# A decoder trunk on one core: an opening in a given order, and a last block that accumulates onto the turned residual stream

## The chip, the cores and the metric

The kernel runs on one core of one Trainium2 chip. The metric is device time in microseconds (us); lower is better. The core has a matrix engine (TensorE, PE in the profile, with its weight loads as PEld), a vector engine (VectorE, DVE), a scalar engine (ScalarE, ACT), GpSimd (POOL), and SyncE (SP), which here only issues transfers. Each engine executes its own list of instructions in order and waits on semaphores for the others; transfers are issued by SP, ACT or POOL and executed by 16 DMA engines. A name such as L1604 is a line of the kernel before. Line numbers in the trace of the changed kernel are its own.

## What is computed

Two layers on one sequence of 512 tokens with 1024 features. Each layer is a gated feed-forward at half weight, a mixer with three kinds of heads, and a second gated feed-forward.

```python
def rms_norm(x, gain):
    xf = x.astype(jnp.float32)
    inv = lax.rsqrt(jnp.mean(xf * xf, axis=-1, keepdims=True) + EPS)
    return (xf * inv).astype(x.dtype) * gain

def swiglu(h, w_in, w_out):
    gate, up = jnp.split(h @ w_in, 2, axis=-1)
    return (jax.nn.silu(gate) * up) @ w_out

for l in range(DEPTH):                                   # 2
    x = x + 0.5 * swiglu(rms_norm(x, ffn1_norm[l]), ffn1_w_in[l], ffn1_w_out[l])
    h = rms_norm(x, mix_norm[l]) @ w_mix_in[l]
    y = ...                                              # short convolution, HGRN2 and FoX heads
    x = x + y @ w_mix_out[l]
    x = x + 0.5 * swiglu(rms_norm(x, ffn2_norm[l]), ffn2_w_in[l], ffn2_w_out[l])
```

The feed-forward is 2816 wide (22 blocks of 128). `hgrn_lb_logits` gives each layer its lower bounds, a small softmax and cumulative sum.

## The kernel before

**Layout and precision.** The residual stream stays on the chip as `xT`, with features on the partitions: 8 slices of 128 features by 512 tokens. Every fp32 matrix product is made of three products of a faster type: an operand is split into a high part (`hi`, a cast on ACT) and a low part (`lo`, a subtraction on DVE), and `mm3` (L308 to L321) issues high by high (L312), high by low (L318) and low by high (L319) into one PSUM bank. So each block of weights passes ACT and DVE before PE can use it. `granule` (L278) loads a pair of weight blocks into `st` (two buffers) and splits them into `hl` (three buffers).

**PSUM.** There are eight banks of 128 by 512 fp32 under four tags: "mm" (3), "sc" (2), "pt" (2), "po" (1). `next4` (L254) gives a group of four in turn: mm, mm, mm, po and sc, sc, pt, pt.

**Order.** A scheduler places the instructions; where `follow` (L272) ties an instruction to the one before it on its engine, the order is as written.

**A feed-forward** (`ffn`, L416) has three parts. First, `covered` of the 22 columns are computed by full products over the 8 slices of x, in groups of two columns, gate and up. Then `halved` runs the remaining columns and two thirds of the output product with seven half-size products in place of eight, on sums of quarters of the weights (`add` and `total` make these, the former by an accumulating transfer from POOL). Last come the six remaining hidden blocks by full products, 72 products for each half of the features.

**The opening.** The first feed-forward of layer 0 covers six columns in three groups (`cover`, L478). In its first group x has to be brought in as well: `open_x` and `load_x` (L1579, L1597) load a slice of x as tokens by features, turn it by four PE transposes into PSUM (L1604), make its high and low parts times the norm's gain (L378, L379), copy it to `xT` (L1594) and add its square to `sqacc` (L389 to L393). The products of the first group do not need the norm's factor `inv`: this is multiplied in after the sum. Behind the first group `build_consts` makes masks on DVE, `lower_bounds` (L923) the lower bounds, and `norm` calls `end_norm` (L403): a product of `sqacc` with a constant matrix on PE (L405) into a bank with the tag "po", a logarithm, an exponential and a square on ACT, and three steps on DVE (L399 to L401). The second group (banks mm, mm, mm, po) needs none of it; the third uses the banks of the first, which `clear` (L529) empties with `inv`. The gain is loaded by SP as 1024 single numbers into 128 partitions (L368). The four loads of weights for the first half-size columns (L823) are issued by SP without regard to the loads of the opening.

**The end.** The last feed-forward writes the output with tokens on the partitions. `turn_x` (L1562) turns `xT` back by 32 PE transposes (L1569) into the "sc" banks, and ACT copies them to SBUF (L1574). The last 144 products go into mm, mm, mm, po and then sc, sc, pt, pt, and for each bank DVE computes 0.5 times the bank plus the turned x (L462), and SP writes 256 KB of the output (L466).

**Tables of ACT.** `table` (L258) loads a table of functions each time that it is called, 15 times in the program.

Of the kernel before, what the change touches and what calls it, by code (L numbers as in the profile page):

```python
# [23 lines left out]
P = 128  # L24
# [132 lines left out]
class Trunk:  # L157
# [8 lines left out]
    def __init__(self, ctx, tc):  # L166
# [20 lines left out]
        self.tab, self.tab_users = None, []  # L187
# [70 lines left out]
    def table(self, name):  # L258
        p = self.nc.scalar.preload_act_table_set(name)
# [18 lines left out]
    def granule(self, parts, kk, ahead=True, skew=0, keep=False):  # L278
# [48 lines left out]
    def stream_steps(self, jobs, parts_of, act, nk, mid=None, pre=None, given=None):  # L327
        k = 0
        while k < nk:
# [7 lines left out]
            rows = self.granule(parts_of(k, kk), kk, pre is None, skew, keep)  # L337
# [78 lines left out]
    def ffn(self, w_in, w_out, next_gain, covered, begin=None, out=None):  # L416
        nc = self.nc
        tc = self.tc
        with tc.tile_pool(name=self.n("ffn"), bufs=1) as fp:
# [4 lines left out]
            self.entry = {}  # L424
            halved = self.halved(fp, w_in, w_out, covered)
# [14 lines left out]
            last = out is not None  # L440
            self.ntog += 1
            if last:
                xs = self.turn_x()
            for dg in range(2):
                banks = self.next4()

                def parts(k, kk, dg=dg):
# [3 lines left out]
                spans = [slice(c, c + P) for c in (0, 128, 256, 384)]  # L451
                self.stream(
                    [
                        (bk, slice(0, T), c) if last else (bk, c, None)
                        for bk, c in zip(banks, spans)
                    ],
                    parts, lambda k: (self.hh[k // 2][:, k % 2, :], self.hl[k // 2][:, k % 2, :]), nf,
                )
                if last:
                    for i in range(4):  # L460
                        o = self.xo[dg * 4 + i]
                        nc.vector.scalar_tensor_tensor(  # L462
                            out=o, in0=banks[i], scalar=0.5, in1=xs[dg * 4 + i],
                            op0=ALU.mult, op1=ALU.add,
                        )
                        nc.sync.dma_start(out[0, spans[i], dg * T : (dg + 1) * T], o)  # L466
                    continue
# [10 lines left out]
    def cover(self, fp, w_in, covered, begin, then):  # L478
        nc = self.nc
        if begin is not None:  # L480
            x, gain, logits = begin
        for f in range(0, covered, 2):
# [8 lines left out]
            def norm():  # L491
                self.end_norm(self.bank("pt" if self.ntog % 2 == 0 else "po"), fp)
                self.xparts = self.halves_of_x(fp)

                for _ in range(2 if begin is not None else 7):
                    next(self.xparts)


            self.stream(
                [(bk, slice(c, c + P), None) for bk, c in zip(banks, (0, 256, 128, 384))],  # L500
                parts, self.xact, KD,
                (2, norm) if opening and begin is None else None,
                (lambda *a: self.open_x(x, gain, fp, *a)) if opening and begin else None,
            )
            if opening and begin is not None:
# [221 lines left out]
    def halved(self, fp, w_in, w_out, covered):  # L727
# [116 lines left out]
        for n, (kind, w, p) in enumerate(seq):  # L844
# [48 lines left out]
            else:  # L893
# [29 lines left out]
    def lower_bounds(self, logits, scratch):  # L923
# [11 lines left out]
        nc.sync.dma_start(lg, logits.rearrange("l (r p) -> p l r", p=P))  # L935
        m = take(2)
        nc.vector.tensor_copy(m, lg[:, 0, :])
# [624 lines left out]
    def turn_x(self):  # L1562
        nc = self.nc
        res, self.xo = [], []
        for h in range(2):
            for i in range(4):
                b = self.bank(("mm", "sc")[self.ntog % 2])
                for q in range(4):
                    nc.tensor.transpose(  # L1569
                        b[:, q * P : (q + 1) * P],  # L1570
                        self.xT[:, h * 4 + q, i * P : (i + 1) * P], self.ident,
                    )
                o = self.res.tile([P, 2, T], F32, tag=f"x{4 * h + i}", name=self.n("xt"))
                nc.scalar.copy(o[:, 0, :], b)  # L1574
                res.append(o[:, 0, :])
                self.xo.append(o[:, 1, :])
        return res

    def open_x(self, x, gain, fp, k, loaded=False):  # L1579
        if not loaded:  # L1580
            if k == 0:
                self.xb = {j: self.load_x(x, j, fp) for j in (0, 1)}
                self.begin_norm(gain)
            for j in (k, k + 1):
                self.norm_part(j, fp, self.xb[j], 0)
            return
        for j in (k + 2, k + 3):
            if j < KD:
                self.xb[j] = self.load_x(x, j, fp)
        for j in (k, k + 1):  # L1590
            self.open_rest(j, fp)

    def open_rest(self, j, fp):
        self.nc.vector.tensor_copy(self.xT[:, j, :], self.xb[j])  # L1594
# [63 lines left out]
```

## Time and profile before

| | us |
|---|---|
| runs shown | 1842.91, 1841.59, 1846.96 (median 1842.91) |
| the profiled execution: its own time | 1837.37 |
| its span, from the first to the last instruction | 1835.6 |
| PE busy in the span | 1815.1 |
| opening: first product of the first group starts | 9.30 |
| opening: first product of the third group starts | 61.23 |
| last block: first transpose to the end of the last product | 1794.39 to 1831.7 |

Views of the profile are quoted in the text. A timeline row gives the start, the time that it took, the engine, the line, the operation, the tiles written and read, the count, and in brackets the engine's idle time before it and what ended it. Rows of one line that follow each other are merged. A matmul's time is longer than the step from one to the next, since they are pipelined: the step between starts is what counts. A row of the list of waits gives who waited, for whom, the total, the number of times and the longest. A row of a tile's or line's groups gives the shortest, median and longest time in nanoseconds.

### The profile page before, as it was taken

The numbers are of one execution on the slowest core, as the hardware profiler recorded it, in microseconds if no ns is written. First come the engines' busy times: TensorE is split into PE (matmuls) and PEld (weight loads), VectorE is DVE, ScalarE is ACT, GpSimd is POOL, SyncE is SP. The second block draws the span as 40 slices with busy tenths as digits, with TensorE's granted clock in tenths as the row PEclk, the third lists the DMA queues.
The fourth block names the chain that finished last, engine by engine and source line by source line (L and its number), as shares of the span: only waits on it lengthen the run. The fifth ranks groups of instructions, "written<-read, shape, count | busy, mean of one in ns | idle before, by whom it ended". The sixth has DMA issues, their size and how long they took to land.

```text
span 1835.6 us, 34734 instructions
## 1 busy us (share of the span) xinstructions
PE 1815.1 (99%) x14328; PEld 1685.2 (92%) x14328; DVE 1459.1 (79%) x2007; ACT 991.8 (54%) x1403; POOL 169.1 (9%) x168
## 2 busy tenths in 40 slices
PE   8999999999999999999999999999999999999999
PEld 6899999899878899999989999998997788999997
DVE  7888887676797888879668887875858878888883
ACT  4455555454675464555445555555547665555552
POOL 0011120100000001112001111201000000020210
PEclk9999999999999999999999999999999999999999
DMA  7659684232322766868266687813233228677762
GB/s 206 169 115 199 172 173 105 75 82 82 87 75 88 216 142 159 183 174 173 70 181 153 159 186 201 167 65 82 76 86 83 76 92 230 160 151 195 152 137 92
DMA packets 244782, 250.94 MB, mean 137 GB/s; under 512 B 19440, under 2 KB 229872, under 8 KB 244624
## 3 DMA queue, kind: packets, MB, share of 16 engines
q1 hardware_dynamic: 191024, 182.64, 32.5%
q0 software_dynamic: 53600, 66.09, 22.3%
q8 instruction: 112, 1.84, 0.4%
q14 instruction: 46, 0.38, 0.1%
HBM read 223.98 MB, written 2.10 MB: 123 GB/s over the span
## 4 chain that ended last, share of the span: by engine, by line
PE 89%; DVE 5%; ACT 3%; issue 1%; DMA 1%; SPq 1%; ACTq 0%
PE mm L312 13%; PE mm L319 13%; PE mm L318 13%; PE sc L319 6%; PE sc L318 6%; PE sc L312 6%; PE pt L312 6%; PE pt L318 6%; PE pt L319 6%; PE po L312 4%; PE po L318 4%; PE po L319 4%; DVE hl L302 1%; PE po L1510 1%; ACT hl L301 1%
## 5 line engine op out<-in xcount | busy, mean ns | idle before, releaser
L771 ACT CAST hl<-w 128x1024 fp32r<-128x1024 f32 x322 | 337.1, 1049 | 321.8 <-PE mm L319 79.0
L773 DVE TENSOR_TENSOR hl<-w,hl 128x1024 fp32r<-128x1024 f32 x322 | 392.8, 1222 | 86.8 <-ACT hl L771 86.6
L302 DVE TENSOR_TENSOR hl<-st,hl 128x512 fp32r<-128x512 f32 (+2 forms) x196 | 166.6, 853 | 119.3 <-ACT hl L301 118.0
L301 ACT CAST hl<-st 128x512 fp32r<-128x512 f32 (+2 forms) x196 | 146.4, 750 | 206.7 <-PE po L319 83.6
L312 PE MATMUL mm<-xc,hl 128*128 128x256 f32 (+1 forms) x732 | 201.5, 276 | 0.5 <-ACT g L882 0.5
L319 PE MATMUL mm<-xc,hl 128*128 128x256 f32 x728 | 201.4, 277 | 0.0
L318 PE MATMUL mm<-xc,hl 128*128 128x256 f32 x728 | 201.4, 277 | 0.0
L319 PE MATMUL sc<-xc,hl 128*128 128x256 f32 x528 | 146.6, 278 | 0.0
L312 PE MATMUL sc<-xc,hl 128*128 128x256 f32 (+1 forms) x530 | 146.6, 277 | 0.0
L318 PE MATMUL sc<-xc,hl 128*128 128x256 f32 x528 | 146.4, 277 | 0.0
L312 PEld LDWEIGHTS mm<-xc,hl 128*128 128x128 f32 x732 | 137.4, 188 | 0.9 <-ACT g L882 0.7
L319 PEld LDWEIGHTS mm<-xc,hl 128*128 128x128 f32 x728 | 136.7, 188 | 0.1
L318 PEld LDWEIGHTS mm<-xc,hl 128*128 128x128 f32 x728 | 136.7, 188 | 0.0
L312 PE MATMUL pt<-xc,hl 128*128 128x256 f32 (+1 forms) x484 | 133.4, 277 | 0.0
L318 PE MATMUL pt<-xc,hl 128*128 128x256 f32 x480 | 133.3, 278 | 0.0
L319 PE MATMUL pt<-xc,hl 128*128 128x256 f32 x480 | 133.0, 277 | 0.0
L312 PE MATMUL mm<-x,hl 128*128 128x512 f32 x272 | 108.9, 401 | 0.8 <-ACT cy L1158 0.8
L319 PE MATMUL mm<-x,hl 128*128 128x512 f32 x272 | 107.6, 395 | 0.0
L318 PE MATMUL mm<-x,hl 128*128 128x512 f32 x272 | 106.7, 392 | 0.0
L318 PEld LDWEIGHTS sc<-xc,hl 128*128 128x128 f32 x528 | 99.6, 189 | 0.0
L312 PEld LDWEIGHTS sc<-xc,hl 128*128 128x128 f32 x530 | 99.5, 188 | 0.2
L319 PEld LDWEIGHTS sc<-xc,hl 128*128 128x128 f32 x528 | 99.1, 188 | 0.1
(485 smaller groups left out, 5611.9 us busy)
## 6 DMA issues: line engine op xcount, KB each, us to landing
w<-in_ffn_w_in_dram SPq DMA_DIRECT2D x140, 512.0 KB
w<-in_ffn_w_out_dram SPq DMA_DIRECT2D x64, 512.0 KB
w<-in_ffn_w_out_dram POOLq DMA_DIRECT2D x56, 512.0 KB, 8.9
st<-in_w_mix_in_dram SPq DMA_DIRECT2D x88, 256.0 KB
st<-in_ffn_w_in_dram SPq DMA_DIRECT2D x72, 256.0 KB
w<-in_ffn_w_in_dram POOLq DMA_DIRECT2D x35, 512.0 KB, 8.4
w<-S POOLq DMA_DIRECT2D x35, 512.0 KB, 4.6
st<-in_ffn_w_out_dram SPq DMA_DIRECT2D x24, 512.0 KB
```

What stands on the lines that cost most here:

```text
L301: a = nc.scalar.copy(hi, src[:, c : c + w])
L302: b = nc.vector.tensor_sub(lo, src[:, c : c + w], hi)
L312: i = nc.tensor.matmul(acc[:, c], ah, bh[:, c], start=first and c.start == 0, stop=False, skip_group_check=True,)
L318: nc.tensor.matmul(acc, ah, bl, start=False, stop=False, skip_group_check=True)
L319: i = nc.tensor.matmul(acc, al, bh, start=False, stop=last, skip_group_check=True)
L771: A(nc.scalar.copy(hi, src))
L773: return lambda: V(nc.vector.tensor_sub(lo, src, hi))
L1510: nc.tensor.matmul(self.ob[:, t0 + u * P : t0 + 2 * P], V[:, j, h % 4].rearrange("p a d -> p (a d)"), part[:, j, u:, :].rearrange("p i t - ...
```

## The change

The opening's first group is written out by a function of its own, `open_stream`, in which `follow` fixes the order on PE, ACT, DVE and SP:

- The gain is loaded by ACT as eight rows of 128 numbers, turned by one PE transpose and copied to SBUF. ACT also issues one of the first weight loads, which are split into four of 128 KB; the second slice of x is loaded behind the first two.
- PE starts with three products of zeros, two more behind the gain's transpose, and two behind the transposes of x's first slice.
- For the first pair of slices the products of the first slice start as soon as its high parts are there (all four high by high first); the second slice is turned behind these four. For later pairs the two next slices are turned in the middle of the pair's products.
- `lower_bounds` stands behind the norm's end instead of before it, and its load and first step are placed in the given order; so are the loads of the second group (`queued`). The weight loads for the first half-size columns come behind these.
- `table` loads nothing if the set is loaded already.

At the end, `way_out` replaces `turn_x` and the last loop: x is turned by transposes that start the banks of the last products, the products accumulate onto it, and DVE copies each bank to SBUF. The factor 0.5 is put into the hidden values of the last six blocks. The last tile is given as two halves of 256 columns: one is copied by DVE and written by SP, the other copied by ACT and written by ACT's queue.

```diff
     def table(self, name):
+        if name == self.loaded:
+            return
+        self.loaded = name
         p = self.nc.scalar.preload_act_table_set(name)
+        if not self.tab_users:
+            self.follow("a", p)
...
     def granule(...):
-            nc.sync.dma_start(s3[:, :, at : at + w], ap.rearrange("(k p) c -> p k c", p=P))
+            d = nc.sync.dma_start(s3[:, :, at : at + w], ap.rearrange("(k p) c -> p k c", p=P))
+            if queued:
+                self.follow("s", d)
...
     def ffn(...):
-            if last:
-                xs = self.turn_x()
+            if out is not None:
+                self.way_out(w_out, out, f0, nf)
+                return
...
-                if last:
-                    for i in range(4):
-                        o = self.xo[dg * 4 + i]
-                        nc.vector.scalar_tensor_tensor(
-                            out=o, in0=banks[i], scalar=0.5, in1=xs[dg * 4 + i],
-                            op0=ALU.mult, op1=ALU.add,
-                        )
-                        nc.sync.dma_start(out[0, spans[i], dg * T : (dg + 1) * T], o)
-                    continue
...
     def cover(...):
+            if opening:
+                self.open_stream(x, gain, fp, parts, jobs)
+            else:
+                self.stream([(*j, None) for j in jobs], parts, self.xact, KD, queued=f == 2)
+            if opening:
                 self.build_consts(...)
+                norm()
                 self.lower_bounds(...)
-                norm()
...
     def halved(...):                       # the last six hidden blocks
-                    V(nc.vector.tensor_mul(y[:, :, H:], pair(g2), pair(u2)))
-                    V(nc.vector.tensor_mul(y[:, :, :H], pair(g1), pair(acc)))
+                    for c, g, v in ((slice(H, T), g2, u2), (slice(0, H), g1, acc)):
+                        if self.final:
+                            V(nc.vector.scalar_tensor_tensor(
+                                out=y[:, :, c], in0=pair(g), scalar=0.5, in1=pair(v),
+                                op0=ALU.mult, op1=ALU.mult,
+                            ))
+                        else:
+                            V(nc.vector.tensor_mul(y[:, :, c], pair(g), pair(v)))
...
+    def way_out(self, w_out, out, f0, nf):
+        nc = self.nc
+        for dg in range(2):
+            banks = self.next4()
+            jobs = []
+            for i, bk in enumerate(banks):
+                t = slice(i * P, (i + 1) * P)
+                for q in range(4):
+                    nc.tensor.matmul(
+                        bk[:, q * P : (q + 1) * P], self.xT[:, dg * 4 + q, t], self.ident,
+                        is_transpose=True, start=q == 0, stop=False, skip_group_check=True,
+                    )
+                cuts = (0, T) if i < 3 or dg == 0 else (0, T // 2, T)
+                jobs += [
+                    (bk[:, a:b], slice(a, b), t, True) for a, b in zip(cuts, cuts[1:])
+                ]
...
+            self.stream(jobs, parts, self.last_hidden, nf)
+            for n, (bk, c, t, _) in enumerate(jobs):
+                o = self.res.tile([P, T], F32, tag=f"x{(4 * dg + n) % 8}", name=self.n("xo"))
+                o = o[:, : c.stop - c.start]
+                if n < 4:
+                    nc.vector.tensor_copy(o, bk)
+                    queue = nc.sync
+                else:
+                    nc.scalar.copy(o, bk)
+                    queue = nc.scalar
+                queue.dma_start(out[0, t, dg * T + c.start : dg * T + c.stop], o)
+
+    def open_stream(self, x, gain, fp, parts, jobs):
...
+        V(nc.vector.memset(zeros, 0.0))
+        A(nc.scalar.dma_start(rows, gain.rearrange("(k p) -> k p", p=P)))
...
+        load(0)
+        w = weights(0)
+        self.table(LNEXP)
...
+        def idle(n):
+            for _ in range(n):
+                E(nc.tensor.matmul(spare[:, :P], zeros, zeros, start=True, stop=True))
+
+        idle(3)
+        E(nc.tensor.transpose(gb[:, :KD], rows, self.ident[:KD, :KD]))
+        A(nc.scalar.copy(self.gain, gb[:, :KD]))
+        idle(2)
+        turn(0)
+        idle(2)
+        for k in range(0, KD, 2):
+            if k:
+                w = weights(k)
+            if k + 2 < KD:
+                load(k + 2)
+                load(k + 3)
...
+            make(0)
+            if k:
+                make(1)
...
+            if k == 0:
+                order = [(n, 0, p) for p in range(3) for n in range(4)]
+                order += [(n, 1, p) for n in range(4) for p in range(3)]
+            elif k + 2 < KD:
+                order = [(n, j, p) for j in range(2) for n in range(4) for p in range(3)]
+            else:
+                order = [(n, j, p) for n in range(4) for j in range(2) for p in range(3)]
+            for i, what in enumerate(order):
+                if k == 0 and i == 4:
+                    turn(1)
+                    make(1)
+                if i == len(order) // 2:
+                    if k + 2 < KD:
+                        turn(k + 2)
+                        turn(k + 3)
+                    for j in (k, k + 1):
+                        nc.vector.tensor_copy(self.xT[:, j, :], xb[j])
+                        self.norm_part(j, fp, xb.pop(j), 1)
+                product(*what)
...
 def trunk_kernel(...):
     k = Trunk(ctx, tc)
-    k.table(LNEXP)
```

In `open_stream`, `load(j)` issues slice j of x on SP, `turn(j)` its four transposes, `weights(k)` the loads of a pair of weight blocks, and `make(j)` the high and low parts of slice j of x and of its weights.

More of the change, by code (lines that the diff above doesn't have):

```diff
@@ L275, in follow, with granule @@
         self.chain[engine] = i.ins.name
-    def granule(self, parts, kk, ahead=True, skew=0, keep=False):
+    def granule(self, parts, kk, ahead=True, skew=0, keep=False, queued=False):
         nc = self.nc
@@ L336, in stream_steps @@
             keep = given is not None and given(k)
[L337 removed]
+            rows = self.granule(parts_of(k, kk), kk, pre is None, skew, keep, queued)
             if keep:
@@ L424, in ffn @@
             self.entry = {}
+            self.final = out is not None
             halved = self.halved(fp, w_in, w_out, covered)
@@ L479, in cover @@
         nc = self.nc
-        if begin is not None:
-            x, gain, logits = begin
+        x, gain, logits = begin
         for f in range(0, covered, 2):
@@ L1560, in fox_attend, with last_hidden @@
             values(*a[1:])
-    def turn_x(self):
+    def last_hidden(self, k):
+        return self.hh[k // 2][:, k % 2, :], self.hl[k // 2][:, k % 2, :]
+    def way_out(self, w_out, out, f0, nf):
         nc = self.nc
-        res, self.xo = [], []
-        for h in range(2):
-            for i in range(4):
[L1567 to L1571, printed above, removed]
-                    )
[L1573 to L1577, printed above, removed]
@@ L1579, in open_x @@
-    def open_x(self, x, gain, fp, k, loaded=False):
-        if not loaded:
-            if k == 0:
[L1582 to L1594, printed above, removed]
-        self.norm_part(j, fp, self.xb.pop(j), 1)
```

87 lines of the change are left out of this document (59 added, 28 removed).

## The prediction

> **What bounds the kernel now.** I read the page first (busy shares, then the chain that ended last).
>
> ```profile
> span 1835.6 us, 34734 instructions
> ...
> PE 1815.1 (99%) x14328; PEld 1685.2 (92%) x14328; DVE 1459.1 (79%) x2007; ACT 991.8 (54%) x1403; POOL 169.1 (9%) x168
> ...
> PE 89%; DVE 5%; ACT 3%; issue 1%; DMA 1%; SPq 1%; ACTq 0%
> ```
>
> TensorE (PE) is busy for 99% of the span and is 89% of the chain, so time can come only out of the stretches in which PE stands or runs slowly. The list of PE's waits says where it stands:
>
> ```profile
> PE mm L1604 <- DMA xs<-in_x_dram: 5.8, 2, 3.8
> PE sc L312 <- DVE gi L534: 1.7, 1, 1.7
> PE po L312 <- DVE nt L399: 1.3, 1, 1.3
> ...
> PE sc L1569 <- ACT xt L1574: 0.4, 1, 0.4
> ```
>
> The first three lie in the opening feed-forward, the fourth in the last one: the stretches that the change rewrites. Between them the changed program has the same instructions in the same order on every engine, but for two table loads (below). So I cost the opening and the end, from the timeline.
>
> ```profile
> 0.76 0.99 SPq L1601 DMA_DIRECT2D xs<-in_x_dram  x2
> ...
> 0.96 0.06 DVE L181 MEMSET epsc<- 128x1 f32 x1
> ...
> 1.79 0.51 SPq L368 DMA_DIRECT2D gain<-in_ffn_norm_dram  x1
> ...
> 3.80 2.09 PE L1604 MATMUL mm<-ident,xs 128*128 128x128 f32 x8 [3.80 <-DMA xs<-in_x_dram]
> ...
> 5.60 0.21 ACT L680 ACTIVATE ngain<-gain 128x8 f32<-128x8 f32 x1 [3.57 <-DMA gain<-in_ffn_norm_dram]
> 5.71 1.25 ACT L378 ACTIVATE x<-mm,gain 128x512 fp32r<-128x512 f32 x2
> ...
> 6.99 1.14 ACT L301 CAST hl<-st 128x512 fp32r<-128x512 f32 x2
> ...
> 7.89 1.12 PE L1604 MATMUL mm<-ident,xs 128*128 128x128 f32 x4 [2.00 <-DMA xs<-in_x_dram]
> ...
> 8.34 1.28 DVE L302 TENSOR_TENSOR hl<-st,hl 128x512 fp32r<-128x512 f32 x2
> ...
> 9.30 0.78 PE L312 MATMUL sc<-x,hl 128*128 128x512 f32 x1
> ...
> 11.15 0.63 PE L312 MATMUL pt<-x,hl 128*128 128x512 f32 x1
> ...
> 11.58 0.63 PE L318 MATMUL pt<-x,hl 128*128 128x512 f32 x1
> ...
> 13.26 0.39 PE L318 MATMUL pt<-x,hl 128*128 128x512 f32 x1
> ...
> 13.49 0.39 PE L319 MATMUL pt<-x,hl 128*128 128x512 f32 x1
> ...
> 19.31 1.03 PE L1604 MATMUL mm<-ident,xs 128*128 128x128 f32 x8
> ...
> 20.10 0.48 PE L312 MATMUL sc<-x,hl 128*128 128x512 f32 x1
> ...
> 1801.09 0.40 PE L312 MATMUL po<-hl,hh 128*128 128x512 f32 x1
> ...
> 1831.50 0.39 PE L319 MATMUL pt<-hl,hh 128*128 128x512 f32 x1
> ```
>
> The first product starts at 9.30. ACT could begin only when the gain was there (5.60), and both slices of x and both halves of the weights were split before any product. A product's step is 0.43 us at 11.15 to 11.58 and 0.23 at 13.26 to 13.49; in the last block 134 steps take 30.41 (1801.09 to 1831.50), 0.227 each. So PE starts at half speed. From 9.30 to 13.49 there are 11 steps: 4.2 instead of 2.5, so the slow start costs 1.7.
>
> **The opening, up to the norm's sum.** Four terms.
>
> (a) The first product comes earlier. x's first slice is still the first transfer and lands at 3.80. On PE stand seven products of zeros, the gain's transpose and x's four. The zeros are written on DVE right after 0.96, so PE begins near 1.3; five of the seven, near 0.47 each (a quarter of the fp32 sum of the norm, 0.94, at half speed), and the gain end by 4.0; the four transposes take 0.9 (the row at 7.89), 4.9. ACT then makes one high part of x (half of 1.25) and one of the weights (half of 1.14), near 6.3, and the product waits for no more: -3.0. Unknown is when the gain lands, now eight rows of 512 bytes from ACT's queue, which issues nothing now, instead of 1024 single numbers from SP's. x took 3.0 from its issue to its use, the gain 3.8 (1.79 to 5.60); issued near 0.8 it lands between 3.0 and 4.6 and would move the product to 7.8 at the latest. I take the early end, because it is the smallest and first on its queue. Bounds -3.2 and -1.5.
>
> (b) Twelve transposes that stood ahead of the first product now stand behind it: 8 take 0.79 (19.31 to 20.10), so +1.2.
>
> (c) The slow start. Full speed came by 13.26, 4.0 after PE's first uninterrupted work at 9.30. A stretch as long from 1.3 on ends at 5.3, before the first product; the zeros are there for this. [...] I take 0.3, nearest to the row: -1.7 + 0.3 = -1.4. [...]
>
> (d) From then on a pair of x's slices needs 24 products (5.45) and 8 transposes (0.8) on PE, and on DVE two low parts of weights (1.28, the row at 8.34) and two low parts of x, copies and sums of squares at about 0.7: 5.5. PE covers it: 0. If that cover goes, PE waits up to 0.5 a pair. Four 512 KB loads of weights for the half-size products, now on SP in the middle of the opening's own loads, are moved behind them and past the second pair of columns' loads; their first user comes 96 full-size products later (21.8), so nothing is late: 0.
>
> Sum up to here: -3.0 + 1.2 - 1.4 = -3.2.
>
> **The norm and the second pair of columns.** PE keeps its order strictly, so it matters where the products into bank "po" stand, which the norm's sum uses as well.
>
> ```profile
> 35.49 1.10 PE L405 MATMUL po<-sqa,ones_mean 128*128 128x512 f32 x2
> ...
> 36.66 0.40 PE L312 MATMUL mm<-x,hl 128*128 128x512 f32 x1
> ```
>
> ```profile
> 36.82 1.05 ACT L301 CAST hl<-st 128x1024 fp32r<-128x1024 f32 x1 [1.12 <-DMA st<-in_ffn_w_in_dram]
> 41.73 0.20 ACT L266 ACTIVATE lb<-lb 128x4 f32<-128x4 f32 x1 [3.86 <-DVE lb L972]
> 41.95 1.28 ACT L259 ACT_TABLE_LOAD   x1
> 43.25 0.69 ACT L266 ACTIVATE nr<-po,epsc 128x512 f32<-128x512 f32 x1
> ```
>
> ```profile
> 39.85 0.23 DVE L950 TENSOR_TENSOR lb<-lb 128x2 f32<-128x2 f32 x2
> ...
> 41.53 0.17 DVE L972 TENSOR_SCALAR lb<-lb 128x4 f32<-128x4 f32 x1
> ...
> 45.30 0.69 DVE L399 SCALAR_TENSOR_TENSOR nt<-po,nt 128x512 f32<-128x512 f32 x1 [3.16 <-ACT nt L266]
> ...
> 60.39 0.69 DVE L534 TENSOR_TENSOR gi<-sc,inv 128x512 f32<-128x512 f32 x1
> ```
>
> The norm's sum is ready at 36.6, but ACT stands 3.86 for the lower bounds (L972) and then loads a table (1.28): its logarithm runs at 43.25, and L399 frees the bank at 46.0. In the new order the norm's logarithm stands ahead of that of the lower bounds, no table is loaded, and only casts of weights stand before it. On the old clock the second of these ends at 37.9 (36.82 + 1.05), 5.4 earlier than 43.25, so the bank is free at 40.6. The small steps of the lower bounds on DVE (39.85 to 41.70, 1.9) and a low part of weights still stand ahead of L399's successor and may push it to 42.0.
>
> But the new order puts "po" right behind the first granule's products into "mm". Of these 13 are left after the sum: 36.66 + 13 x 0.227 = 39.6. PE waits there 1.0 to 2.4, and all the rest of its work stands behind; I take 1.8. The wait for gi goes: 78 products follow (17.7), so PE comes to "sc" at 59.1, while gi ends 15.1 after L399 does (46.0 to 61.1, in nearly the same order), at 55.7 to 57.1. Removed 1.7 + 1.3 (the list of waits), added 1.8: -1.2, bounds -2.5 and +1.
>
> **The end.**
>
> ```profile
> 1794.39 1.04 PE L1569 MATMUL sc<-ident,xT 128*128 128x128 f32 x8
> ```
>
> ```profile
> L1574 ACT COPY xt<-sc x8: 578/585/589, 1795.9 to 1800.6; 128x512 f32<-128x512 f32 x8
> L466 SPq DMA_DIRECT2D out_dram<-xt x8: 332/333/360, 1813.1 to 1832.6; - x8
> ...
> L462 DVE SCALAR_TENSOR_TENSOR xt<-pt,xt x2: 692/692/692, 1830.6 to 1831.9; 128x512 f32<-128x512 f32 x2
> ```
>
> PE's last stretch is 1794.39 to 1831.73, 37.3 us. The new one has the same 32 transposes (0.1 each, 3.2) and 144 products (32.7; the halves are half as long), some 0.1 at each of four changes between them, and perhaps 0.15 for the last "mm" bank: 36.4. What goes is the wait of 0.4 for ACT's copies and the alternation with them: -0.9, bounds -1.3 and -0.3. The eight copies themselves (0.585) ran beside PE: 0.
>
> Behind the last product stand 0.69 on DVE, 0.33 of issue on SP and 2.66 to the span's end for 256 KB. The last tile now goes in halves to DVE and ACT, but the program's waits put them one behind the other: the DVE copy waits for all twelve products, ACT's for DVE's. [...] A half costs about 0.4 on either (a little over half of 0.69 and of 0.585): 0.8 against 0.69. The last transfer has half the bytes:
>
> ```profile
> 9.30:13.00 3.70, 3.70 (x11) 2.98 (x10) 2.28 (x4) 1.03 (x2) 0.00 (x0) 1.00 1.16 335
> ```
>
> At those 335 GB/s (last column) it is 0.4 shorter. An issue by ACT is not in the trace; I take SP's 0.33 to 0.51. Together -0.1, bounds -0.6 and +0.5. The factor 0.5 goes into a DVE product of the same shape: 0.
>
> **Table loads.** Two more go (1.28 each), at the norms ahead of the second feed-forwards. PE's first products there cover them: its list of waits is empty from 590 to 680 and from 1500 to 1590. Taken as 0; without that cover 1.28 each.
>
> **Sum.** -3.2 - 1.2 - 0.9 - 0.1 = -5.4, made against the profiled execution's own time of 1837.37 (1.8 around its span): 1832.0. The median of the runs shown is 5.5 higher, 1842.91, and I carry the difference over: 1837.5.
>
> **Rivals.**
>
> 1. Zeros and transposes don't raise the clock. For: the transposes at 3.80 and 7.89 raised nothing. Against: between those PE stood for 2.00, and the zeros are ordinary products. [...]
>
> 2. Slower: "po" holds PE's whole line. What else is gained makes 3.2 + 3.0 + 1.0 = 7.2, so the change loses from a wait of 7.2 on, a bank that is free at 46.8 on the old clock. Were ACT's chain to keep its distance (46.0) and 2.5 of DVE's small steps and low parts to come ahead of L399's successor, it would be 48.5: +1.7, 1844.6. For: the casts ahead of the logarithm wait for transfers. Against: the 3.86 and the 1.28 are gone from ACT's order.
>
> 3. More: the bank is free before PE comes to it, and the clock is up at 6.3 (1.8 + 0.3), with 0.3 more at the end: -7.8, 1835.1. For: only transfers hold the chain. Against: DVE's steps ahead of L399's successor.
>
> **Chances.** The forecast 0.58, the rivals 0.2, 0.06 and 0.16. 0.3% is 5.5 us, about what a measurement of this kernel can tell. The forecast's own range is 1836.0 to 1839.0, with its middle at that bound, so about half of it is faster: 0.3 + 0.16 and a little of the first rival, 0.48. Slower by so much (1848.4) is more than the second rival has: 0.03. Within: 0.49. The range takes in the third rival, most of the first, and the runs' scatter: 1834.6 to 1841.6.
>
> **What would show it.** The first product near 6.3 (a), with steps of 0.23 from the start (c); the norm's logarithm 1 to 2 behind its sum, a wait of about 1.8 at the first "po" product and none at "sc"; no ACT copies of x in the last block, which takes 36.4, and its two half copies one behind the other. I am wrong if products still take 0.43 at 10 us, if the "po" wait is over 4, or if PE waits for DVE's low parts in the opening.

## The result and the profile after

The changed kernel takes 1836.75 us (median of 15 runs, 1831.88 to 1842.45) against 1842.91 of the kernel before (15 runs, 1837.40 to 1848.81). The ratio is 0.997, 95% interval 0.9957 to 0.9982: a gain of 3.3 to 7.9 us, 5.5 by the ratio. The profiled execution takes 1832.22 with a span of 1830.4, 5.2 less than the span before.

The page of the changed kernel, its busy shares and its chain:

```profile
PE 1817.7 (99%) x14361; PEld 1689.5 (92%) x14361; DVE 1459.7 (80%) x2008; ACT 983.3 (54%) x1394; POOL 169.1 (9%) x168
...
PE 93%; DVE 4%; ACT 2%; issue 1%; DMA 0%; SPq 0%; ACTq 0%; DVEq 0%
```

PE has 93% of the chain instead of 89%. Its list of waits, in the form of the one before:

```profile
PE mm L1650 <- DVE z L1638: 1.2, 1, 1.2
...
PE sc L1676 <- ACT hl L1632: 0.4, 1, 0.4
...
PE sc L1676 <- DVE x L386: 0.2, 1, 0.2
```

The four waits that the prediction started from are gone from it. What the opening still has is 1.2 ahead of PE's very first instruction, 0.4 ahead of the first product and 0.2 for a low part of x. The timeline of the changed kernel, from the first zeros to the third group:

```profile
1.22 1.65 PE L1650 MATMUL mm<-z 128*128 128x128 f32 x6 [1.22 <-DVE z L1638]
...
2.80 0.27 PE L1653 MATMUL po<-ident,gr 8*128 8x8 f32 x1
...
4.02 1.06 PE L1613 MATMUL mm<-ident,xs 128*128 128x128 f32 x4
...
6.36 1.14 PE L1676 MATMUL sc<-x,hl 128*128 128x512 f32 x2 [0.43 <-ACT hl L1632]
7.34 0.62 PE L1676 MATMUL pt<-x,hl 128*128 128x512 f32 x2
7.81 0.60 PE L1613 MATMUL mm<-ident,xs 128*128 128x128 f32 x4
...
28.59 0.50 PE L1676 MATMUL sc<-x,hl 128*128 128x512 f32 x1 [0.16 <-DVE x L386]
...
33.75 1.02 PE L412 MATMUL po<-sqa,ones_mean 128*128 128x512 f32 x2
...
37.37 0.39 PE L326 MATMUL mm<-x,hl 128*128 128x512 f32 x1
37.76 0.50 PE L319 MATMUL po<-x,hl 128*128 128x512 f32 x1
...
55.57 0.39 PE L319 MATMUL sc<-x,hl 128*128 128x512 f32 x1
```

The first product starts at 6.36 (9.30 before). The first two pairs of products start at 6.36 and 7.34, 0.98 apart for two products, and the next two take 0.47 (7.34 to 7.81): two slow steps, then full speed. The norm's product is at 33.75, the first product into "po" follows the last into "mm" by 0.39, and the third group starts at 55.57, without a wait. Before, it started at 61.23. The opening has gained 5.66.

At the end, the same view:

```profile
1789.69 1.60 PE L1572 MATMUL mm<-ident,xT 128*128 128x128 f32 x12
...
1826.21 0.28 PE L326 MATMUL pt<-hl,hh 128*128 128x256 f32 x1
1826.53 0.42 DVE L1590 COPY xo<-pt 128x256 f32<-128x256 f32 x1 [0.74 <-PE pt L326]
...
1826.98 0.37 ACT L1593 COPY xo<-pt 128x256 f32<-128x256 f32 x1 [17.81 <-DVE xo L1590]
1827.39 0.34 ACTq L1595 DMA_DIRECT2D out_dram<-xo  x1
```

From the first transpose to the span's end the last block takes 40.71 (1789.69 to 1830.4). Before it took 41.21 (1794.39 to 1835.6). ACT's copy is released by DVE's, as the row's bracket says. So the two stages that were rewritten give 5.66 + 0.5 = 6.2. The difference of the medians is 6.16; that the two agree so closely is luck, since the measurement leaves 3.3 to 7.9 open. The profiled pair shows only 5.2 because it differs in the middle too, where both programs have the same order; this is taken up in the last section.

### The profile page after: what moved, and what is told of

It reads as the page before. It is cut to its first block, busy times and chain, and to the rows that moved or that the text cites. A ratio compares the mean times of both kernels' runs of the same rounds, so it can differ in the third digit from the quotient of the medians.

```text
span 1830.4 us, 34800 instructions
## 1 busy us (share of the span) xinstructions
PE 1817.7 (99%) x14361; PEld 1689.5 (92%) x14361; DVE 1459.7 (80%) x2008; ACT 983.3 (54%) x1394; POOL 169.1 (9%) x168
## 4 chain that ended last, share of the span: by engine, by line
PE 93%; DVE 4%; ACT 2%; issue 1%; DMA 0%; SPq 0%; ACTq 0%; DVEq 0%
PE mm L319 14%; PE mm L326 13%; PE mm L325 13%; PE sc L326 6%; PE sc L325 6%; PE sc L319 6%; PE pt L325 6%; PE pt L326 6%; PE pt L319 6%; PE po L319 4%; PE po L325 4%; PE po L326 4%; PE po L1509 1%; PE pt L1550 1%; PE pt L1244 1%
## 5 line engine op out<-in xcount | busy, mean ns | idle before, releaser
L309 DVE TENSOR_TENSOR hl<-st,hl 128x512 fp32r<-128x512 f32 (+2 forms) x188 | 161.5, 860 | 118.6 <-ACT hl L308 117.2
L308 ACT CAST hl<-st 128x512 fp32r<-128x512 f32 (+2 forms) x188 | 141.9, 755 | 207.1 <-PE po L326 82.4
```

The costliest lines, as they stand in the source:

```text
L308: a = nc.scalar.copy(hi, src[:, c : c + w])
L309: b = nc.vector.tensor_sub(lo, src[:, c : c + w], hi)
```

## The experiments

All are edits of the changed kernel. The first of four stage times below is the start of the first product, then come those of the norm's product and of the third group, and the stretch from the last block's first transpose to the span's end. Each row is read from one trace. Where runs share the opening of the changed kernel (changed, two_banks, whole_tile, opening_only, opening_timed), the norm's product agrees within 0.05 and the third group within 0.3; the seven edits that keep its end have the last block between 40.77 and 40.83. Spans are given to 0.1.

| | first product | norm | third group | last block |
|---|---|---|---|---|
| before | 9.30 | 35.49 | 61.23 | 41.21 |
| changed | 6.36 | 33.75 | 55.57 | 40.71 |
| no_zeros | 5.98 | 34.07 | 56.36 | 40.80 |
| turned_zeros | 6.45 | 34.51 | 56.31 | 40.83 |
| more_zeros | 6.36 | 33.93 | 55.91 | 40.81 |
| low_behind | 6.42 | 32.67 | 56.13 | 40.80 |
| masks_pool | 6.36 | 35.96 | 57.79 | 40.78 |
| old_norm | 6.41 | 33.71 | 57.68 | 40.81 |
| copy_act | 6.59 | 32.95 | 55.30 | 40.77 |
| two_banks | 6.36 | 33.74 | 55.66 | 40.27 |
| whole_tile | 6.36 | 33.74 | 55.85 | 40.62 |
| opening_only | 6.62 | 33.71 | 55.83 | 41.70 |
| both | 6.37 | 32.98 | 55.32 | 40.29 |
| opening_timed | 6.36 | 33.70 | 55.83 | 41.75 |

Five products of the second group stand ahead of the norm's product in the changed kernel, none in low_behind, three in copy_act and both, so for the norm's product low_behind is to be raised by 1.13 and the other two by 0.45 (0.227 a product) to be compared with the changed kernel. Before, two stand there.

**What raises the clock, and what it is worth.** Three runs change PE's work ahead of the first product.

```diff
# no_zeros
-        idle(3)
+        idle(0)
...
-        idle(2)        (twice)
+        idle(0)
# turned_zeros
-            for _ in range(n):
-                E(nc.tensor.matmul(spare[:, :P], zeros, zeros, start=True, stop=True))
+            for _ in range(2 * n):
+                E(nc.tensor.transpose(spare[:, :P], zeros, self.ident))
# more_zeros
         turn(0)
-        idle(2)
+        idle(4)
```

> The changed kernel without its seven products of zeros; all else stays. Measure: the start of the third group's first product (55.57 in the changed kernel, 61.23 before) and PE's steps from the first product on. [...] Rival (the five transposes and the first products do as much, or the clock rises at a time of its own): steps as in the changed kernel, third group at 55.6.

> The changed kernel with each product of zeros replaced by two transposes of zeros, which keep PE busy for the same time. Theory (whatever keeps PE busy raises the clock): as in the changed kernel, half-speed steps for about two products, third group at 55.4 to 56.0. [...]

> The changed kernel with four products of zeros in place of two behind x's first four transposes, so that PE doesn't stand between 5.72 and 6.36. Theory A (the pause ahead of the first product delays the clock): full steps from the first product on, first product at 6.4 to 6.6, third group at 55.2 to 55.5. Theory B (the clock rises at the end of a period that the pause doesn't matter to): two or three half-speed steps again, third group at 55.6 to 55.8.

The timeline of no_zeros:

```profile
3.58 1.11 PE L1613 MATMUL mm<-ident,xs 128*128 128x128 f32 x4 [0.82 <-DMA xs<-in_x_dram]
5.98 1.22 PE L1676 MATMUL sc<-x,hl 128*128 128x512 f32 x2 [1.28 <-ACT hl L1632]
7.00 1.05 PE L1676 MATMUL pt<-x,hl 128*128 128x512 f32 x2
...
8.56 1.11 PE L1676 MATMUL sc<-x,hl 128*128 128x512 f32 x2
9.50 0.63 PE L1676 MATMUL pt<-x,hl 128*128 128x512 f32 x2
```

Its steps stay slow until 9.4, 3.4 after the first product, which costs half of that, 1.7, so the rival falls. But the third group comes only 0.8 later than in the changed kernel (56.36), and the norm's product only 0.3 later. The slow start was not free, but little of it arrived: the first product came 0.38 earlier without the zeros ahead of it, the wait of 0.16 for DVE at 28.59 is gone, and 0.47 is a wait at "po" for DVE's nt (L406), behind the norm. The timeline of turned_zeros:

```profile
1.52 1.54 PE L1650 MATMUL mm<-ident,z 128*128 128x128 f32 x6 [1.52 <-POOL ident masks.py:199]
...
4.96 1.06 PE L1650 MATMUL mm<-ident,z 128*128 128x128 f32 x4
6.45 0.74 PE L1676 MATMUL sc<-x,hl 128*128 128x512 f32 x2 [0.43 <-ACT hl L1632]
7.03 0.63 PE L1676 MATMUL pt<-x,hl 128*128 128x512 f32 x2
...
9.07 0.74 PE L1676 MATMUL sc<-x,hl 128*128 128x512 f32 x2 [0.98 <-DVE x L386]
```

PE has done nothing but transposes, and the first product is at full speed (6.45 to 7.03 for two). So here transposes raise the clock. The third group is late all the same (56.31), for another reason: PE waits 0.98 for DVE's low part of x at 9.07. In more_zeros the first product is at full speed too (6.36 to 6.93 for two), and the third group comes at 55.91, not earlier than in the changed kernel. Both of its theories fall: the clock was up in time, and it bought nothing.

That is the pattern of all runs with this opening. By the trace's record of the granted clock, full speed came at 5.25 (two_banks), 5.33 (opening_timed), 5.93 (opening_only), 7.28 (changed) and 7.75 (whole_tile), and the norm's product stands at 33.74, 33.70, 33.71, 33.75 and 33.74. The latest of these rises costs PE some 0.7 after the first product ((7.75 - 6.36) / 2), and none of it shows. Over this range something that doesn't depend on PE's clock sets the norm's product; in no_zeros, with the rise at 9.42, it is at 34.07.

**DVE in the opening.** The view of the stretch from 6 to 34 (columns: the stretch, its length, busy time of PE, PEld, DVE, ACT and POOL with counts, granted clock, DMA share, GB/s), first of the kernel before, then of the changed one, then of copy_act (the record of the granted clock begins with its first rise, so the view has 1.00 ahead of it too):

```profile
6.00:34.00 28.00, 26.11 (x116) 21.57 (x117) 24.21 (x55) 14.83 (x26) 1.44 (x1) 1.00 0.85 248
```

```profile
6.00:34.00 28.00, 27.45 (x130) 22.40 (x131) 27.14 (x63) 15.16 (x27) 0.00 (x0) 1.00 0.57 164
```

```profile
6.00:34.00 28.00, 27.31 (x130) 21.88 (x131) 24.50 (x68) 19.68 (x36) 0.00 (x0) 1.00 0.59 169
```

In the changed kernel DVE is busy for 27.14 of 28. Its groups in that stretch show with what (line, engine, operation, tiles, shape, count, busy time, mean in ns, idle time before):

```profile
L1633 DVE TENSOR_TENSOR hl<-st,hl 128x512 fp32r<-128x512 f32 x8 | 5.4, 679 | 0.0
...
L309 DVE TENSOR_TENSOR hl<-st,hl 128x1024 fp32r<-128x1024 f32 x2 | 2.4, 1222 | 0.3 <-ACT hl L308 0.3
L238 DVE TENSOR_TENSOR lmask<-c,c 64x64 uint8<-64x64 f32 x10 | 2.2, 218 | 0.2
```

The first row is one of the four kinds of work on the pairs of slices that the prediction counted (the others: sums of squares 4.8, x's low parts 5.9, copies 5.4). The low parts of the second group's weights (2.4) and the masks (2.2 in the last row, and 3.5 in three smaller groups of compares and products) it didn't count. (The rows add up to 29.6, more than 27.14, since the steps overlap in part: in the timeline the one at 6.45 takes 0.22, and the next starts at 6.59.) Three runs move work there.

```diff
# low_behind: the first low part of the second group behind those of x's last slice
+            if self.behind:
+                self.tc.add_manual_dep(b.ins, self.behind, NOSYNC, reason="given order")
# masks_pool: the two compares and the product of each of six masks
-            nc.vector.tensor_scalar(a, xf, scalar1=float(2 ** (l - 1)), ...)
+            nc.gpsimd.tensor_scalar(a, xf, scalar1=float(2 ** (l - 1)), ...)
# copy_act
-                        nc.vector.tensor_copy(self.xT[:, j, :], xb[j])
+                        nc.scalar.copy(self.xT[:, j, :], xb[j])
```

> The changed kernel, with the low part of the second group's first weights (1.22 on DVE, 26.65) placed behind the low parts of x's last slice. Theory (the waits of 0.74 in all at 27.5 to 28.9 come from this order on DVE): they shrink to 0.2 or less, the norm's product comes 1 to 1.7 earlier than 33.75 since no product of the second group stands ahead of it, a wait of up to 0.4 for bank po may come back, and the third group starts at 55.0 to 55.3. Rival (DVE has too much work there in any order, or transfers are late): PE waits 0.5 or more at the last pair of slices, third group at 55.5 or later.

> The changed kernel with 18 of the small steps that build the masks (two compares and a product for each of six masks, 0.22 to 0.29 each on DVE) given to GpSimd. Theory (DVE, busy for 27.1 of the 28 us from 6 to 34, limits the opening beside PE): DVE falls to about 23, the waits of 0.74 at the last pair of x's slices go, and the third group starts at 54.4 to 55.1 instead of 55.57. Rival (transfers or ACT set these waits): PE still waits 0.5 or more there, third group at 55.5 or later.

> The changed kernel with the eight copies of x's slices to xT (0.68 each) on ACT, which is busy for 15.2 of the 28 us from 6 to 34, instead of DVE (27.1 of 28). Theory (DVE, not the clock, is what sets the opening's pace beside PE): DVE falls to about 22.5, PE's waits at the last pair (0.74) shrink to 0.2 or less, the norm's product, counted at the same number of products before it, comes 0.5 to 0.9 earlier, and the third group starts at 54.6 to 55.2. Rival (the copies stand ahead of the high parts on ACT, and these come late): new waits for ACT at the pairs' starts, third group at 55.6 or later.

low_behind goes to its rival. The norm's product is at 32.67, and with the five products that no longer stand ahead of it at 33.81: DVE's work has another order, but as much of it (26.61 of the 28), and PE waits as long. The third group is 0.56 later than in the changed kernel, because PE waits 0.51 at "po" for DVE's nt. masks_pool misses both its theory and its rival. Its DVE is freer (24.35 of the 28), but the steps of the masks that stay on DVE now wait for GpSimd. From the timeline of masks_pool:

```profile
5.71 0.46 POOL L235 TENSOR_TENSOR c<-c,c 128x128 f32<-128x128 f32 x1
...
8.00 0.45 DVE L238 TENSOR_TENSOR lmask<-c,c 64x64 uint8<-64x64 f32 x2 [1.34 <-POOL c L235]
8.48 0.75 DVE L386 SCALAR_TENSOR_TENSOR x<-mm,gain,x 128x512 fp32r<-128x512 f32 x1
```

A step that takes 0.22 to 0.29 on DVE takes 0.46 and more on GpSimd, DVE stands 1.34 in its order, x's low part (8.48) with it and PE for 1.3 behind that: the third group comes at 57.79. It says nothing for or against DVE's load as the limit. copy_act speaks for it. With 2.6 less on DVE (the copies are 5.4, but other work moved into the stretch) the norm's product is at 32.95 + 0.45 = 33.40 instead of 33.7, though its first product was 0.23 later, and the third group starts at 55.30, where the runs with this opening have 55.57 to 55.85. That is half of the gain I expected, and short of its range (54.6 to 55.2): PE is nearly as full as DVE (27.3 of 28), so little is left to win.

**The norm and bank "po".** This run undoes two edits at once, the order of the norm and the lower bounds and the skipped table loads, since they belong together: in the kernel's code each load of a table is tied behind all functions since the last one (`table`), so a load between the lower bounds and the norm's logarithm keeps the two in this order. No run undoes one of them alone.

```diff
# old_norm
-        if name == self.loaded:
-            return
...
-                norm()
                 self.lower_bounds(...)
+                norm()
```

> The changed kernel with the old order of the lower bounds and the norm, and with a table loaded at each call as before; the opening's first group and the end stay. The program then has six products into mm ahead of the first into po. Theory (the early norm is what took the wait for po away): the logarithm runs 3.5 to 4 later than at 34.95, PE waits 2 to 3 at its first product into po, and the third group starts at 57.4 to 58.4. Rival (PE reaches po late enough, or DVE holds it anyway): wait under 1, third group at 55.5 to 56.5. The two further table loads at the norms ahead of the second feed-forwards: no wait on PE in either.

ACT in the changed kernel and in old_norm, from the timelines:

```profile
34.00 1.04 ACT L308 CAST hl<-st 128x1024 fp32r<-128x1024 f32 x1 [1.43 <-PE pt L1676]
34.95 0.68 ACT L271 ACTIVATE nr<-po,epsc 128x512 f32<-128x512 f32 x1
```

```profile
37.28 0.20 ACT L269 ACTIVATE lb<-lb 128x4 f32<-128x4 f32 x1 [2.15 <-DVE lb L969]
37.50 1.28 ACT L260 ACT_TABLE_LOAD   x1
38.80 0.69 ACT L269 ACTIVATE nr<-po,epsc 128x512 f32<-128x512 f32 x1
```

The logarithm runs 3.85 later, of which 1.28 is the load itself, and the third group starts at 57.68 instead of 55.6 to 55.8. PE's list of waits in old_norm has it in two places:

```profile
PE sc L317 <- DVE gi L525: 1.3, 1, 1.3
...
PE po L317 <- DVE nt L404: 0.7, 1, 0.7
```

The total is as expected (57.4 to 58.4), but its split isn't: 0.7 at "po", where I had 2 to 3, and a wait for gi that I had not named. The list has no wait at the norms ahead of the second feed-forwards, where two more tables are loaded.

**The end.**

```diff
# two_banks
+                split = i == 3 and dg == 1
+                bks = [bk, self.bank("mm") if split else bk]
...
-                        bk[:, q * P : (q + 1) * P], ...
+                        bks[q // 2][:, q * P : (q + 1) * P], ...
# whole_tile
-                cuts = (0, T) if i < 3 or dg == 0 else (0, T // 2, T)
+                cuts = (0, T)
# opening_only: turn_x and the last loop of the kernel before, no factor in the hidden values
```

> The changed kernel with the second half of the last tile in a bank of its own (mm), so that the two copies need not follow each other. From the first transpose of the last block to the span's end the changed kernel takes 40.7 (1789.69 to 1830.4), and 4.2 from its last product's start. Theory (the two copies stand one behind the other because they share a bank): the DVE copy runs beside the last products, 3.7 to 3.9 from the last product's start, 40.2 to 40.4 in all. Rival (the writes of the earlier tiles set the end): 4.1 to 4.2, 40.6 to 40.8.

> The changed kernel with the last tile in one piece: 512 columns, copied by DVE and written by SP. Theory (the split costs what it saves: its 36 half products step at 0.119 instead of 0.1135, and its copies follow each other): as before the change 4.1 from the last product's start, and 40.2 to 40.5 from the first transpose of the last block to the end. Rival (the half transfer gains 0.4, as I reckoned): 4.4 to 4.6 and 40.9 to 41.2.

> The changed opening and tables with the end of the kernel before. Theory (the two parts don't touch each other): third group at 55.5 to 55.9 as in the changed kernel, and from the first transpose of the last block to the span's end 41.0 to 41.4 as in the kernel before, against 40.7 to 40.8. Rival (part of the end's gain belongs to the opening's tables or the factor of 0.5): under 40.9.

The last rows of two_banks:

```profile
1829.34 0.42 DVE L1594 COPY xo<-pt 128x256 f32<-128x256 f32 x1
...
1829.74 0.28 PE L326 MATMUL mm<-hl,hh 128*128 128x256 f32 x1
...
1830.06 0.37 ACT L1597 COPY xo<-mm 128x256 f32<-128x256 f32 x1 [17.35 <-PE mm L326]
```

The DVE copy is done before the last product has ended, and ACT waits for PE alone. The span ends 3.76 after the last product's start (4.19 in the changed kernel), and the block takes 40.27. whole_tile takes 40.62, 0.1 to 0.2 less than the split in one bank. From the first transpose to the end of the last product it takes 36.35 (its last start 36.12 later, and 0.23) against 36.64 (36.52 and 0.12), and from there 4.27 against 4.07. So the split loses 0.3 on PE and gains 0.2 behind it; the first theory is right in sign, and wrong in the tail, which I expected at 4.1 from the last start and is at 4.51.

opening_only takes 41.70, above the expected 41.4, and opening_timed 41.75, though their end is that of the kernel before, which takes 41.21. What grew lies behind the last transfer. These are the stretches from the end of the last transfer to the end of the span, of the kernel before, of opening_only and of the changed kernel:

```profile
1834.28:1835.60 1.32, 0.00 (x0) 0.00 (x0) 0.00 (x0) 0.00 (x0) 0.00 (x0) 0.94 0.00 0
1827.11:1828.80 1.69, 0.00 (x0) 0.00 (x0) 0.00 (x0) 0.00 (x0) 0.00 (x0) 0.95 0.00 0
1828.76:1830.40 1.64, 0.00 (x0) 0.00 (x0) 0.00 (x0) 0.00 (x0) 0.00 (x0) 0.88 0.00 0
```

No engine computes there and nothing is moved (last column). This closing of the program takes 1.32 before and 1.64 to 1.69 after, with the old end as well as with the new one. So 0.3 to 0.4 of the last block of every changed run does not come from the edits of the end; which part of the change brings it, no run shows. It is also why the tail of whole_tile is 4.51 and not 4.1. Against opening_only and opening_timed, which have the longer closing too, the whole end is worth 0.9 to 1.0.

**Together, and timed.**

> The changed kernel with the copies to xT on ACT and the second half of the last tile in a bank of its own. Theory (the two gains add up): third group at 55.0 to 55.5, 40.2 to 40.4 from the first transpose of the last block to the span's end, about 0.8 less than the changed kernel in all, which makes a ratio to the kernel before of 0.9965 where the changed kernel had 0.997 (0.9957 to 0.9982). Rival (the clock's phase and the end's transfers swallow it): the stages as in the changed kernel, 55.6 and 40.75 or more. The ratio alone can't tell the two apart.

> The changed opening and tables with the end of the kernel before, timed in five rounds. Theory (the opening carries all but half a microsecond or so of the gain): ratio to the kernel before 0.9965 to 0.9978. Rival (the end carries a third or more, 2 us): 0.998 or more.

Both has the stages that were expected (55.32 and 40.29) and a ratio of 0.9971 (0.9957 to 0.9985) to the kernel before, 1831.40 against 1837.05. opening_timed has 0.9966 (0.9951 to 0.9982) and 1833.19. Neither can be told from the changed kernel's 0.997: the intervals are 5 us wide, and these edits move the stages by 0.3 to 1.0. What opening_timed shows is that the opening alone carries a gain of 3.3 to 9.0; a third of it in the end is not excluded by the ratio. By the stage times it is less: the end brings 0.5 of 6.2 against the kernel before, and 0.9 to 1.0 against the same opening with the old end.

## Why the prediction was right, step by step

The forecast was 1837.5 and 1832.0 for the profiled execution; 1836.75 and 1832.22 came out. The sum of the two stages was -5.4 and is -6.2. Its terms did less well than the sum: two of them are off by 0.8 and 2.0, in opposite directions, so that the sum came so close is in part luck.

- **(a) first product, -3.0:** right, 6.36. The gain was on PE by 2.80, a little before the earliest that I had reckoned with (3.0). No run separates what each part brings to it: the gain's new load, the new order, and the weight loads that were moved out of the way.
- **(b) transposes behind it, +1.2:** right but for one. Sixteen transposes turn the first four slices. In the kernel before fifteen of them stood ahead of the first product (twelve in the rows at 3.80 and 7.89, three in the first row here), and the last one ran at 13.72. In the changed kernel four still stand ahead of it, so eleven moved: 1.1. If my twelve were the rows at 3.80 and 7.89, two slips cancel, since four of those still stand ahead.

```profile
8.80 0.85 PE L1604 MATMUL po<-ident,xs 128*128 128x128 f32 x3
...
13.72 0.27 PE L1604 MATMUL po<-ident,xs 128*128 128x128 f32 x1
```

- **(c) slow start, -1.4:** the two slow steps are there (0.5 lost, 0.3 forecast: -1.2). No run shows the 0.3, which was an estimate: the changed kernel lost 0.5, and no_zeros 1.7. Transposes did count for the clock (in turned_zeros PE did nothing else ahead of 6.45, and then two products in 0.58). But the clock isn't worth what the term says: without any zeros, with the slow start back, the third group comes only 0.5 to 0.8 later. The slow start of the first rival was brought about in no_zeros, and this was its price, not the 1.7 that PE lost.
- **(d) "PE covers it: 0":** this step failed. I took DVE's work for a pair of slices as 5.5 and left out the masks (5.7 in all) and the second group's low parts (2.4). DVE is busy for 97% of the stretch, and the norm's product stays at 33.7 for rises of the clock from 5.25 to 7.75. PE does wait for a low part of x (28.59), which the prediction had named as a sign of being wrong. The gaps at 27.5 to 28.9 make 0.74. Like for like (98 products ahead of the norm's before, 101 now) the first group gained 1.74 + 0.68 = 2.4 instead of 3.2; the four terms as measured, -2.9 + 1.1 - 1.2 + 0.7, make -2.3.
- **The wait at "po", +1.8:** mis-sized, 0.17. I had the logarithm behind two casts, at 36.2 by the new clock, and up to 1.4 more for DVE's small steps. It ran at 34.95, behind one cast, and most of these steps had run on DVE by the time that ACT had done its three functions (36.96). So the third rival's first half came true: the bank is free as PE comes to it. That the waits for nt and gi (3.0) would go was right, and old_norm shows that it hangs on the early logarithm: 2.0 of the opening's gain.
- **The end, -0.9 and -0.1:** -0.7 from the first transpose to the end of the last product (37.34 to 36.64). The half products step at 0.119 instead of 0.1135, which is the 0.2 that is missing on PE. Behind the last product it is +0.2 (3.87 to 4.07), because the closing of the program is 0.3 to 0.4 longer; the sum had no term for that. Without it, that part would be near the -0.1 that was forecast. That the two copies follow each other was right (ACT's at 1826.98 is released by DVE's), and that it is because they share a bank, two_banks shows: there PE releases ACT's.
- **Table loads, 0:** right.

So the opening's first group gave less than forecast because DVE became the limit beside PE (0.8 less), its second group gave 2.0 more because "po" was free in time, and the end gave 0.5 less, so the sum came out 0.8 over the forecast. The rival on the slower side, "po" holding PE's line, did not come about even in old_norm.

## What to carry to other kernels

When a change fills one engine's gaps, add up all that the next engine has in that stretch, with the small work that the scheduler had tucked into its idle time; here 8 us of masks and low parts made DVE the limit, and of the 1.7 that a slow start costs on PE only 0.5 to 0.8 reached the third group. A table load can cost more than its 1.3 us by the order that it keeps: here, together with the old order of the calls, it held a logarithm 3.85 later, behind a chain of small steps on another engine. And splitting the last tile paid here only with the halves in different banks (0.3 to 0.4 over the whole tile): in one bank the copies stood in line, and the smaller products cost 0.1 to 0.2 more than the shorter transfer brought. When the time behind the last product changes, look first whether the closing of the program did: 0.3 to 0.4 of it here belongs to no edit of the end.

## What the runs showed of the hardware

PE's clock drops in the middle of the program. The stretches view of the changed kernel at two places and right behind the first:

```profile
399.81:403.22 3.41, 3.29 (x16) 3.29 (x16) 3.41 (x4) 0.60 (x1) 0.00 (x0) 0.50 0.02 5
403.22:406.63 3.41, 3.41 (x32) 3.41 (x31) 2.49 (x5) 1.30 (x3) 0.00 (x0) 1.00 0.12 18
1304.34:1307.76 3.42, 3.42 (x19) 3.42 (x18) 3.42 (x4) 0.60 (x1) 0.00 (x0) 0.50 0.02 5
```

For exactly 3.41 the granted clock is 0.50 (the eighth number) and PE does 16 products instead of 32. Both starts lie a whole number of 3.41 behind the opening's rise at 7.28 (115 and 380 periods of 3.413); the rise itself comes at 5.25 to 7.75 in the runs with this opening. Each such drop costs about 1.5: 16 and 19 products are done where some 30 fit at 0.113 each. The traces of the changed kernel and its edits have one to three of them, the one trace of the kernel before none. But the kernel before has them too: a drop takes 0.001 off a run's mean granted clock (half of 3.41 in 1830; the trace with two has 0.998), and of the 20 runs of the kernel before that were timed beside both and opening_timed, 14 have 0.999, three 0.998, one 0.997 and only two 1.000. Of the 15 runs of the changed kernel eight have 0.999, five 0.998 and two 0.997. By these figures that is 1.2 drops a run before and 1.6 after, an estimate.

There is a second slowdown, with the granted clock at 1.00. The same 100 us of both kernels:

```profile
700.00:800.00 100.00, 100.00 (x853) 100.00 (x852) 81.42 (x84) 49.56 (x56) 16.58 (x14) 1.00 0.71 162
```

```profile
700.00:800.00 100.00, 100.00 (x885) 100.00 (x884) 84.34 (x87) 54.34 (x62) 16.58 (x14) 1.00 0.78 175
```

Before (first) PE did 853 half-size products, after 885: 0.117 each against 0.113, which makes 3.6 in these 100 us. Other executions have such stretches too, of 20 to 110 us, not all of them at the same places. What causes them stays open. They and the drops of the clock are of the size of the difference of 1 in the middle of the two profiled executions; added up over all half-size products, the time of each step above 0.113 makes some 10 before and 8 after, and the two drops take 3, so the changed kernel should be 1 longer there, as it is. The runs of one kernel scatter by 11 us.
